# Recurrent branch of a hybrid block: products 512 and 256 wide, halves added on two engines

## The chip, the cores and the metric

The kernel runs on one core of a Trainium2 chip, for one layer at 256 tokens and width 2048, in float32. The metric is device time in microseconds. All weights come from HBM in each execution. Engines: TensorE (PE) multiplies, VectorE (DVE) and ScalarE (ACT) work elementwise, SyncE (SP) issues nearly all transfers.

## The reference, cut to what matters

```python
def rg_lru(x, w_a, b_a, w_i, b_i, lam):
    r = sigmoid(einsum('btnd,nde->btne', xb, w_a) + b_a)
    i = sigmoid(einsum('btnd,nde->btne', xb, w_i) + b_i)
    log_a = (8.0 * r) * log_sigmoid(lam)
    a = exp(log_a)
    b = sqrt(-expm1(2.0 * log_a)) * (i * x)
    return scan(h_t = a_t * h_{t-1} + b_t)

z = rmsnorm_mod(x) @ w_in         # q, kc, vc, ks, vs, kw, vw, gates, lx, ly, ga, gb
o_a = nsa_attention(...)
u = causal_dwconv(lx, conv_w, conv_b)            # 4 taps
o_b = gelu(ly) * rg_lru(u, w_a, b_a, w_i, b_i, lam)
merged = sigmoid(ga) * (o_a @ proj_a) + sigmoid(gb) * (o_b @ proj_b)
x = x + g1 * (merged @ w_out)
x = x + g2 * conv_glu_ffn(rmsnorm_mod(x))
```

The six vectors that scale, shift and gate come from `silu(c) @ ada_w`, 12288 columns wide.

## The kernel before, in words

Every float32 product is made of three products of rounded parts. A weight tile is split into `hi`, its rounded copy, written by ScalarE (L107), and `lo`, the rest, written by VectorE (L108); the activations lie in SBUF as 512 columns, 256 of rounded values and then 256 of the rest. The sum is hi with both halves and lo with the first. Weights come in tiles `raw` of 128 x 2048 (1 MB, four buffers, loaded through `stage`, L97, on SP's queue in program order). Each is split in two parts of 1024 columns; `hi` and `lo` have three buffers each. One such part is called a half below.

`dense_pair` (L114), used in the up projection, multiplies hi with all 512 columns at once and lo with 256, and a reduction adds the two halves of the accumulator. `dense_pair1` (L172), used for the recurrent branch, makes three products 256 wide (L185, L187, L188) into half a bank, so that one bank holds the two finished tiles of a call and no addition is needed. There are four banks `P` (tag "d").

The program order near the change is as follows. After the projections for attention, eight calls of `dense_pair1` compute `lx` (L721), each followed by an attention unit while any is left and by two pieces of the modulation (`filler(2)`, L726; a piece is one 1 MB load of `ada_w` and one 2048-wide VectorE operation, L234). ScalarE copies each accumulator into `lx` (L722), whose four buffers are the slots C4 to C7; C7 holds a tile of attention until its last unit.

Then come four blocks of the recurrence (L731), 512 channels each. A block makes the convolution `u` on VectorE (L746 the first tap, L749 the others), the gate products (L751, L753), sigmoids (L757, L758), a multiplication by -4 log_sigmoid(lam) on VectorE (L759), tanh (L761), exp (L762) and square root (L763) on ScalarE, three VectorE operations (L764 to L766), and the scan (L768). Two calls of `dense_pair1` per block then compute `ly`; ScalarE takes gelu from the accumulator into the slot of `u` (L773), VectorE multiplies with the scan's result (L774), and the product is split into `oB` (L777, L778).

The merge (L787) multiplies attention and recurrence by `proj_a` and `proj_b` in four groups of columns, with two fillers per product in the first group and four in the others (L803).

A scheduler orders each engine's instructions by a timeline of its own. `tc.high_priority` moves instructions forward, `tbl` keeps the order of ScalarE's functions that need tables, and the loads stay in program order. What an engine runs is the fixed order that results: an instruction that waits holds up those behind it.

## Time and profile before

| | us |
|---|---|
| median of three runs | 1794.22 (1793.13 to 1794.91) |
| the profiled execution | 1792.45 |
| its span, first to last instruction | 1790.7 |
| attention's last units and `lx`, about | 318 to 465 |
| recurrence and `ly`, about | 465 to 592 |
| merge, from | 592 |

In the profile, "PE P L188 <- DVE lo L108: 0.8, 2, 0.7" reads: TensorE's instructions of line 188 waited for VectorE's line 108 for 0.8 us in all, twice, at most 0.7. In a list of groups the columns are line, engine, operation, tiles and shapes, count, then busy time in us and mean duration in ns, then the idle time of the engine before it. In a timeline they are start, duration, engine, line. In the rows of the instruction order there is no time.

### The profile page before, as it was taken

The numbers are of one execution on the slowest core, as the hardware profiler recorded it, in microseconds if no ns is written. First come the engines' busy times: TensorE is split into PE (matmuls) and PEld (weight loads), VectorE is DVE, ScalarE is ACT, GpSimd is POOL, SyncE is SP. The second block draws the span as 40 slices with busy tenths as digits, with TensorE's granted clock in tenths as the row PEclk, the third lists the DMA queues.
The fourth block names the chain that finished last, engine by engine and source line by source line (L and its number), as shares of the span: only waits on it lengthen the run. The fifth ranks groups of instructions, "written<-read, shape, count | busy, mean of one in ns | idle before, by whom it ended". The sixth has DMA issues, their size and how long they took to land.

```text
span 1790.7 us, 25736 instructions
## 1 busy us (share of the span) xinstructions
PE 1769.6 (99%) x10254; PEld 1544.8 (86%) x10254; DVE 1350.7 (75%) x1978; ACT 883.1 (49%) x1204; POOL 0.2 (0%) x4
## 2 busy tenths in 40 slices
PE   8999999999999999999999999999999999999998
PEld 7899898888999888888888998888888888888886
DVE  7999897998698766767665997888555666777555
ACT  5644464655578444444445644444433444444443
POOL 0000000000000000000000000000000000000000
PEclk8999999999999999999999999999999999999999
DMA  9989864665555867777775566777655555555552
GB/s 348 379 330 364 289 248 157 236 212 208 215 177 223 305 236 291 284 292 282 293 265 198 186 233 237 282 282 282 236 193 200 193 188 190 188 188 188 189 193 112
DMA packets 64344, 429.50 MB, mean 240 GB/s; under 512 B 7104, under 2 KB 7392, under 8 KB 15840
## 3 DMA queue, kind: packets, MB, share of 16 engines
q1 hardware_dynamic: 63936, 427.08, 66.1%
q8 instruction: 80, 1.31, 0.3%
q10 hardware_dynamic: 288, 0.79, 0.1%
q14 instruction: 40, 0.33, 0.0%
HBM read 425.72 MB, written 2.11 MB: 239 GB/s over the span
## 4 chain that ended last, share of the span: by engine, by line
PE 93%; DVE 3%; DMA 1%; ACT 1%; issue 1%; SPq 0%; DVEq 0%; ACTq 0%
PE P L130 26%; PE P L204 12%; PE P L205 12%; PE P L203 12%; PE P L187 3%; PE P L188 3%; PE P L185 3%; PE P L470 2%; PE P L471 2%; PE P L472 2%; PE P L149 1%; PE P L464 1%; PE P L148 1%; PE P L465 1%; PE P L150 1%; PE P L463 1%
## 5 line engine op out<-in xcount | busy, mean ns | idle before, releaser
L107 ACT ACTIVATE hi<-raw 128x1024 fp32r<-128x1024 f32 x588 | 622.1, 1060 | 764.2 <-PE P L205 320.8
L108 DVE TENSOR_TENSOR lo<-raw,hi 128x1024 fp32r<-128x1024 f32 x588 | 717.0, 1222 | 370.6 <-ACT hi L107 369.7
L130 PE MATMUL P<-h,hi 128*128 128x512 f32 x1344 | 463.9, 394 | 0.0
L130 PE MATMUL P<-h,lo 128*128 128x256 f32 x1344 | 366.4, 278 | 0.0
L130 PEld LDWEIGHTS P<-h,hi 128*128 128x128 f32 x1344 | 249.1, 188 | 54.9
L130 PEld LDWEIGHTS P<-h,lo 128*128 128x128 f32 x1344 | 252.4, 188 | 4.2
L234 DVE SCALAR_TENSOR_TENSOR raw<-raw,crow 128x2048 f32<-128x2048 f32 x64 | 146.2, 2284 | 3.3 <-DMA raw<-ada_w 3.1
L188 PE MATMUL P<-h,lo 128*128 128x256 f32 x512 | 147.6, 289 | 0.8 <-DVE lo L108 0.8
L187 PE MATMUL P<-h,hi 128*128 128x256 f32 x512 | 146.8, 287 | 0.0
L185 PE MATMUL P<-h,hi 128*128 128x256 f32 x512 | 146.8, 287 | 0.0
L470 PE MATMUL P<-h,hi 128*128 128x256 f32 x384 | 108.0, 285 | 0.0
L471 PE MATMUL P<-h,hi 128*128 128x256 f32 x384 | 107.9, 285 | 0.0
L472 PE MATMUL P<-h,lo 128*128 128x256 f32 x384 | 102.2, 283 | 0.0
L188 PEld LDWEIGHTS P<-h,lo 128*128 128x128 f32 x512 | 97.8, 191 | 1.8 <-DVE lo L108 1.4
L187 PEld LDWEIGHTS P<-h,hi 128*128 128x128 f32 x512 | 97.9, 191 | 1.4 <-issue 1.2
L185 PEld LDWEIGHTS P<-h,hi 128*128 128x128 f32 x512 | 97.9, 191 | 1.0 <-issue 0.7
L204 PE MATMUL P<-lo,ua 128*128 128x512 f32 x240 | 93.4, 389 | 0.0
L205 PE MATMUL P<-hi,ua 128*128 128x512 f32 x240 | 93.4, 389 | 0.0
L203 PE MATMUL P<-hi,ua 128*128 128x512 f32 x240 | 83.6, 389 | 0.0
L204 PE MATMUL P<-lo,h 128*128 128x512 f32 x192 | 75.4, 393 | 0.2 <-DVE lo L108 0.2
L205 PE MATMUL P<-hi,h 128*128 128x512 f32 x192 | 74.9, 390 | 0.0
L470 PEld LDWEIGHTS P<-h,hi 128*128 128x128 f32 x384 | 74.2, 193 | 0.5 <-issue 0.4
(285 smaller groups left out, 3131.0 us busy)
## 6 DMA issues: line engine op xcount, KB each, us to landing
raw<-w_up SPq DMA_DIRECT2D x96, 1024.0 KB, 4.8
raw<-ada_w SPq DMA_DIRECT2D x94, 1024.0 KB, 4.9
raw<-w_down SPq DMA_DIRECT2D x48, 1024.0 KB, 4.8
raw<-w_lru SPq DMA_DIRECT2D x32, 1024.0 KB, 4.9
raw<-w_proj SPq DMA_DIRECT2D x32, 1024.0 KB, 5.1
raw<-w_gates SPq DMA_DIRECT2D x24, 1024.0 KB, 6.4
raw<-w_out SPq DMA_DIRECT2D x16, 1024.0 KB, 4.9
raw<-w_kv SPq DMA_DIRECT2D x24, 512.0 KB, 7.2
```

Of the source, the lines that this page charges most:

```text
L107: A.activation(hi[:, :n], raw[:, lo_col:lo_col + n], AF.Copy)
L108: V.tensor_tensor(lo[:, :n], raw[:, lo_col:lo_col + n], hi[:, :n].bitcast(F32), op=ALU.subtract)
L130: PE.matmul(ps[f][:, 0:256] if w else ps[f], hl[w][:, k * 256 + f * 128:k * 256 + f * 128 + 128], r[:, 0:256] if w else r, start=(kt == 0 ...
L185: PE.matmul(o, hi[:, sl], r[:, 0:256], start=(kt == 0 and f == 0), stop=False, skip_group_check=True)
L187: PE.matmul(o, hi[:, sl], r[:, 256:512], start=False, stop=False, skip_group_check=True)
L188: PE.matmul(o, lo[:, sl], r[:, 0:256], start=False, stop=(kt == n - 1), skip_group_check=True)
L203: PE.matmul(ps[j], xh, hi[:, w], start=(kt == 0), stop=False, skip_group_check=True)
L204: PE.matmul(ps[j], xh, lo[:, w], start=False, stop=False, skip_group_check=True)
L205: PE.matmul(ps[j], xl, hi[:, w], start=False, stop=(kt == n - 1), skip_group_check=True)
L234: V.scalar_tensor_tensor(raw, raw, 1.0, row, op0=ALU.mult, op1=ALU.mult, accum_out=modc[:, c:c + 1])
L470: PE.matmul(o, hi[:, sl], h1[:, kt, 0:256], start=first and f % 2 == 0, stop=False, skip_group_check=True)
L471: PE.matmul(o, hi[:, sl], h1[:, kt, 256:512], start=False, stop=False, skip_group_check=True)
```

## The change

Line numbers in the text on the changed kernel are its own; behind the change of `dense_pair1` they lie one to seven above those of before.

- `dense_pair1` makes one product 512 wide (L184) and one 256 wide (L185) per tile into a bank of its own, two banks per call.
- `add_halves`, new, copies the second half of each bank on ScalarE (L192) and adds the first on VectorE (L193), at high priority.
- `lx` lies in C4, C5, C6 and D0; the gelu of `ly` has a slot of its own (C0 to C7, later that of `oB`) and not that of `u`; the temporaries of the recurrence move to other slots.
- The convolution's first tap moves to ScalarE (L753).
- The multiplication by -4 log_sigmoid(lam) goes into the scale of tanh (L766), and exp becomes four instructions with a scale of 8 log_sigmoid(lam) (L768); `lsp8` (L606) is that vector.
- The gelu works in SBUF, and the product with the scan's result is written over the latter.
- After each `lx` call one or two fillers run, 12 in all and not 16; in the merge's first group four per product and not two.

```diff
         def dense_pair1(pieces, rhs):
-            p = bank()
+            ps = [bank(), bank()]
...
-                        o = p[:, f * 256:f * 256 + 256]
...
-                            PE.matmul(o, hi[:, sl], r[:, 0:256], start=(kt == 0 and f == 0), stop=False,
+                            PE.matmul(ps[f], hi[:, sl], r, start=(kt == 0), stop=False, skip_group_check=True)
+                            PE.matmul(ps[f][:, 0:256], lo[:, sl], r[:, 0:256], start=False, stop=(kt == n - 1),
                                       skip_group_check=True)
-                            PE.matmul(o, hi[:, sl], r[:, 256:512], start=False, stop=False, skip_group_check=True)
-                            PE.matmul(o, lo[:, sl], r[:, 0:256], start=False, stop=(kt == n - 1),
-                                      skip_group_check=True)
-            return p
+            return ps
+
+        def add_halves(dst, ps):
+            with tc.high_priority(200):
+                for f in range(2):
+                    A.activation(dst[:, f], ps[f][:, 256:512], AF.Copy)
+                    V.tensor_tensor(dst[:, f], ps[f][:, 0:256], dst[:, f], op=ALU.add)
...
+            lsp8 = lz
+            V.tensor_scalar(lsp8, ls, 8.0, None, op0=ALU.mult)
...
-        lx = [big.tile([128, 4, T], F32, tag="C%d" % (4 + n), name="lx") for n in range(4)]
+        lx = [big.tile([128, 4, T], F32, tag=t_, name="lx") for t_ in ("C4", "C5", "C6", "D0")]
...
-            A.activation(lx[pr // 2][:, 2 * (pr % 2):2 * (pr % 2) + 2],
-                         pl.rearrange("p (f t) -> p f t", f=2), AF.Copy)
+            add_halves(lx[pr // 2][:, 2 * (pr % 2):2 * (pr % 2) + 2], pl)
             if units:
                 attention(*units.pop(0))
-            filler(2)
+            filler(1 + pr % 2)
...
-                    V.tensor_scalar(uf, x, col("lcw", 48 + b), col("lcb", b), op0=ALU.mult, op1=ALU.add)
+                    A.activation(uf, x, AF.Identity, bias=col("lcb", b), scale=col("lcw", 48 + b))
...
-                V.tensor_scalar(r[:, n], r[:, n], lsm4[:, b:b + 1], None, op0=ALU.mult)
-                if n % 2:
-                    tbl(A.activation(tt[:, n - 1:n + 1], r[:, n - 1:n + 1], AF.Tanh))
-            tbl(A.activation(r, r, AF.Exp, scale=-2.0))
+                tbl(A.activation(tt[:, n], r[:, n], AF.Tanh, scale=lsm4[:, b:b + 1]))
+            for n in range(4):
+                tbl(A.activation(r[:, n], r[:, n], AF.Exp, scale=lsp8[:, bt * 4 + n:bt * 4 + n + 1]))
             tbl(A.activation(tt, tt, AF.Sqrt))
...
-                gl = u[:, 2 * h:2 * h + 2]
-                tbl(A.activation(gl, pl.rearrange("p (f t) -> p f t", f=2), AF.Gelu_apprx_tanh))
-                V.tensor_tensor(gl, gl, iu[:, 2 * h:2 * h + 2], op=ALU.mult)
+                gl, hs_ = big.tile([128, 2, T], F32, tag="C%d" % pr, name="gl"), iu[:, 2 * h:2 * h + 2]
+                add_halves(gl, pl)
+                tbl(A.activation(gl, gl, AF.Gelu_apprx_tanh))
+                V.tensor_tensor(hs_, gl, hs_, op=ALU.mult)
...
-                filler(2 if n == 0 else 4)
+                filler(4)
```

Two places of the order on the engines that the prediction speaks of: on ScalarE, in a block of the recurrence, where the splits of weights (`hi<-raw`) stand between its functions (`lt`; L761 tanh, L762 exp, L763 root, L773 gelu), before, in the third block:

```order
L107 ACTIVATE hi<-raw 128x1024 x2
L761 ACTIVATE lt<-lt 128x512
L762 ACT_TABLE_LOAD
L762 ACTIVATE lt<-lt 128x1024
L763 ACT_TABLE_LOAD
L763 ACTIVATE lt<-lt 128x1024
L107 ACTIVATE hi<-raw 128x1024
L773 ACT_TABLE_LOAD
L773 ACTIVATE lt<-P 128x512
```

and in the first block of the changed kernel (L768 exp, L753 first taps of a later block, L769 root, L780 gelu, L764 and L765 sigmoids):

```order
L768 ACT_TABLE_LOAD
L768 ACTIVATE lt<-lt,lz 128x256 x3
L753 ACTIVATE lt<-lx,cols 128x256 x4
L768 ACTIVATE lt<-lt,lz 128x256
L769 ACT_TABLE_LOAD
L769 ACTIVATE lt<-lt 128x1024
L780 ACT_TABLE_LOAD
L780 ACTIVATE gl<-gl 128x512 x2
L764 ACT_TABLE_LOAD
L764 ACTIVATE lt<-lru_r,cols 128x256
L765 ACTIVATE lt<-lru_i,cols 128x256
L107 ACTIVATE hi<-raw 128x1024
```

The gelus (L780) and the next block's first sigmoids (L764, L765), each with a table load, and four first taps moved ahead of the split. On SP's queue (loads by tile and source) the pieces of `ada_w` in the merge's first group become four per product; before:

```order
L53 DMA raw<-w_proj 128x2048 x4
L53 DMA raw<-ada_w 128x2048 x2
L53 DMA raw<-w_proj 128x2048 x4
L53 DMA raw<-ada_w 128x2048 x2
L53 DMA raw<-w_gates 128x2048 x4
```

and after:

```order
L53 DMA raw<-w_proj 128x2048 x4
L53 DMA raw<-ada_w 128x2048 x4
L53 DMA raw<-w_proj 128x2048 x4
L53 DMA raw<-ada_w 128x2048 x4
L53 DMA raw<-w_gates 128x2048 x4
```

The four pieces that left the `lx` loop stand behind the two products of this group.

## The prediction

> **What bounds the kernel now.** I read the page first, then busy time by stage, then the waits of TensorE, and last the timelines of TensorE and ScalarE where the change acts.

> ```profile
> span 1790.7 us, 25736 instructions
> PE 1769.6 (99%) x10254; PEld 1544.8 (86%) x10254; DVE 1350.7 (75%) x1978; ACT 883.1 (49%) x1204; POOL 0.2 (0%) x4
> PE 93%; DVE 3%; DMA 1%; ACT 1%; issue 1%; SPq 0%; DVEq 0%; ACTq 0%
> ```

> TensorE is the bound nearly everywhere. Busy time on that engine is modelled, so what matters is the pitch from one product's start to the next. The stages, with columns us, PE, PEld, DVE, ACT, POOL, clock, DMA share and GB/s, are the recurrence's inputs beside attention (318 to 465), the recurrence proper (465 to 592), and the first part of the merge:

> ```profile
> 318.00:465.00 147.00, 146.51 (x1023) 124.24 (x1022) 131.14 (x356) 87.81 (x217) 0.00 (x0) 1.00 0.60 211
> 465.00:592.00 127.00, 126.18 (x948) 120.71 (x947) 104.05 (x142) 93.56 (x123) 0.00 (x0) 1.00 0.59 213
> 592.00:650.00 58.00, 58.00 (x261) 48.02 (x261) 38.91 (x45) 24.36 (x26) 0.00 (x0) 1.00 0.72 267
> ```

> VectorE is 89% busy in the first of them, ScalarE 74% in the second. TensorE waits there, in all, for this:

> ```profile
> PE tp L695 <- ACT pcT L667: 0.5, 1, 0.5
> PE P L188 <- DVE lo L108: 0.8, 2, 0.7
> ```

> These are 1.3 us, so removing waits can bring little. ScalarE, on the other side, still has slack in the recurrence: it mostly waits for TensorE to free one of the three `hi` buffers.

> ```profile
> ACT hi L107 <- PE P L187: 17.3, 13, 3.3
> ```

> **The products.** One pair of tiles now takes three 256-wide products, and afterwards one of 512 and one of 256, the form that the up projection (L130) has today. Columns are start, duration, line and operation:

> ```profile
> 524.48 0.28 PE L185 MATMUL P<-h,hi 128*128 128x256 f32 x1
> ...
> 525.92 0.28 PE L185 MATMUL P<-h,hi 128*128 128x256 f32 x1
> 1400.13 0.39 PE L130 MATMUL P<-h,hi 128*128 128x512 f32 x1
> ...
> 1403.94 0.40 PE L130 MATMUL P<-h,hi 128*128 128x512 f32 x1
> ```

> From 524.48 to 525.92 are four rounds of three: 1.44/4 = 0.360 us. From 1400.13 to 1403.94 are eleven rounds of two: 3.81/11 = 0.3464 us. The columns streamed are the same; what goes is one instruction, 13.6 ns. There are 512 rounds (16 calls, 16 row tiles, 2 halves), so the products save 512 x 0.0136 = 7.0 us, all on the path. [...]

> The two accumulators per call take two of the four banks, so a call's first product waits for the sums of the call before last. A call lasts 32 x 0.3464 = 11.1 us and each sum is put ahead in both queues: I cost that at nothing, and at 1 us a call if the cover goes.

> **VectorE.** The rows for what goes and comes (busy, then mean ns):

> ```profile
> L234 DVE SCALAR_TENSOR_TENSOR raw<-raw,crow 128x2048 f32<-128x2048 f32 x64 | 146.2, 2284 | 3.3 <-DMA raw<-ada_w 3.1
> L746 DVE TENSOR_SCALAR lt<-lx,cols 128x256 f32<-128x256 f32 x16 | 5.8, 407 | 0.3 <-PE s L673 0.3
> L759 DVE TENSOR_SCALAR lt<-lt,lsm 128x256 f32<-128x256 f32 x16 | 5.3, 347 | 2.1 <-ACT lt L757 1.9
> L161 DVE TENSOR_TENSOR gp<-P,rB 128x256 f32<-128x256 f32 x6 | 2.4, 416 | 0.0
> ```

> Gone are 5.8 and 5.3 us, added are 32 sums at 0.416 = 13.3 us, and four modulation pieces (9.1 us) leave the attention stage for the merge. In the attention stage VectorE is relieved by some 5 us (16 sums against four pieces and a few taps). That is worth the 0.5 us wait there, no more.

> **ScalarE is where I see the price.** It gets 32 copies, 16 first taps and 16 separate exponentials. How they are ordered matters more than their sum. In the two pieces of its queue shown with the change, a split of weights (`hi`, L107) came right behind the root; after, the closing split stands behind the root, two gelus and the next block's first sigmoids, and four taps stand among the exponentials. Two more such runs follow, in blocks 1 and 2. The rows that price them:

> ```profile
> 543.37 0.61 ACT L761 ACTIVATE lt<-lt 128x512 f32<-128x512 f32 x1
> 544.00 1.28 ACT L762 ACT_TABLE_LOAD   x1
> 545.29 1.06 ACT L762 ACTIVATE lt<-lt 128x1024 f32<-128x1024 f32 x1
> 546.36 1.28 ACT L763 ACT_TABLE_LOAD   x1
> 547.65 1.06 ACT L763 ACTIVATE lt<-lt 128x1024 f32<-128x1024 f32 x1
> 548.62 1.04 ACT L107 ACTIVATE hi<-raw 128x1024 fp32r<-128x1024 f32 x1
> 549.68 1.28 ACT L773 ACT_TABLE_LOAD   x1
> L349 ACT ACTIVATE nt<-xbuf,modc 128x256 f32<-128x256 f32 x14 | 8.2, 588 | 0.0
> L298 ACT ACTIVATE h<-nt,modc 128x256 fp32r<-128x256 f32 x18 | 8.7, 500 | 5.5 <-DVE nt L304 5.1 <-DVE nt L876 0.3
> L906 ACT ACTIVATE ua<-fv 128x256 fp32r<-128x256 f32 x32 | 12.1, 418 | 1.5
> L757 ACT ACTIVATE lt<-lru_r,cols 128x256 f32<-128x256 f32 x16 | 7.7, 479 | 0.9 <-PE lru_r L751 0.9
> L814 ACT ACTIVATE mg<-turn 128x256 fp32r<-128x256 f32 x16 | 5.2, 377 | 2.8 <-PE turn L812 2.8
> ```

> A table load stands 1.29 us before its successor (544.00 to 545.29), a 1024-wide operation 0.97 (547.65 to 548.62), so a queued activation about 0.1 us less than its duration. Taking 0.1 off the others: a tap, which has a bias and a scale per partition as L349 has, 0.49; a tanh or exp with a scale per partition 0.40 as L298 (bounds 0.32 by L906, which has none, and 0.49 by L349); a sigmoid 0.37; a copy of a half sum 0.28 by L814. The rows shown of after, the closing split included, so take 12.5 us, against 6.3 for those of before (543.37 to 549.68). [...]

> TensorE's cover is three split halves: 16 products, 8 x 0.3464 = 2.77 us each. The last of the three is handed over 1 us after the buffer came free. The plain sum over the stretch from the last attention product to the end of the third run, ten splits by the order of after:

> - ScalarE: 10 splits at 0.97, 10 table loads at 1.29, 23 sigmoids at 0.37, 24 tanh and exp at 0.40, 12 taps at 0.49, 3 roots at 0.97, 6 of 512 at 0.53, 7 copies at 0.28, one output copy 0.5: 9.7 + 12.9 + 8.5 + 9.6 + 5.9 + 2.9 + 3.2 + 2.0 + 0.5 = 55.2 us.
> - TensorE meanwhile: 12 halves, 33.3 us; 20 gate products and 4 of attention's:

> ```profile
> 521.77 0.60 PE L751 MATMUL lru_r<-lt,raw 128*128 128x256 f32 x2
> 522.21 0.59 PE L753 MATMUL lru_i<-lt,raw 128*128 128x256 f32 x2
> 470.56 3.44 PE oT L703 x8
> ```

> A gate product is two records, 0.44 us (521.77 to 522.21); attention's four are the 3.44. Together 33.3 + 8.8 + 3.4 = 45.5, less the 1 us of the first hand-over, 44.5.

> The difference, 10.7 us, is time in which TensorE has no split weights. With the bounds of the new activations (24 at 0.32 or 0.49, taps at 0.40) it is 7.7 to 12.9; sums that wait in VectorE's queue behind a late `lo` may add up to 4. The same reckoning for before gives some 28 us of ScalarE work in ten splits, far below TensorE's; only the 6.3 us run comes near three halves, and the larger of the two waits, 0.7 us, is what it costs. In the last block the runs are 4.6, 2.6, 2.8 and 6.7 us against halves of 2.77: 16.7 against 11.1 and the cover of some 4: I put 2 us (0 to 3.5).

> **The moved pieces.** As SP's queue shows, four loads of 1 MB join the merge's first group, ahead of loads of weights. In the 58 us from 592 VectorE is busy 38.91, 67%, and with 9.1 us more 83%; transfers go from 267 GB/s to about 267 + 4.2 MB/58 us = 340. Both leave room, less in the group itself, which is shorter. I take 0.5 us (0 to 2.3).

> **Sum.** Against the profiled execution, 1792.45 us with a span of 1790.7: -7.0 (products) -1.3 (waits that go) +10.7 +2 +0.5 = +4.9, so 1797.4. The median of the three runs, 1794.22, lies 1.8 above that execution: **1799.2 us**.

> **The rivals.**

> - *Faster: the runs on ScalarE are covered.* It holds if the three halves and the gate products hide each run, so that the second stage waits no more than now. For it: the 17.3 us that ScalarE itself waits for TensorE today. Against it: that slack lies between runs, and 55.2 against 44.5 leaves none. It decides where all new waits together stay below 4.7 us (8.3 less 3.6). With none, 1794.2 - 8.3 = 1786. Chance 0.15.
> - *No change: the shortfall is half of my sum.* New activations at their cheap bound, the last block covered: -8.3 + 7.7 = -0.6, so 1793 to 1795. Chance 0.22.
> - *Slower still: VectorE's order adds to it.* Half sums, taps of the next block and a modulation piece stand ahead of a `lo` whose products are already late, and the merge starts with VectorE behind: -8.3 + 12.9 + 4 + 2.3 = +11, so 1805. Chance 0.13.

> **How the numbers follow.** The forecast has 0.50, at 1799.2. About 0.2% (3.6 us) is what a measurement of this kernel can tell from no change: 1790.6 to 1797.8. Faster is the first rival, 0.15; same the second and nothing else, 0.22; slower the rest, 0.63. The range leaves out half of the first rival and the top of the last: 1788 to 1806.

> **What would show it.** Pitch of L184 to L184 at 0.346 us. Waits of TensorE for `hi` L107 or `lo` L108 in the second stage near 10 us in three or four places, each behind a run of table loads on ScalarE, where before there were 0.8. No wait for the sums at L193. The attention stage shorter by 4 us. If those waits stay below 3 us in all, the forecast is wrong and the first rival right.

## The result, and the profile after

The changed kernel takes **1814.71 us** (median of four runs, 1811.90 to 1817.39), the kernel before, run beside it, 1794.05 (1793.13 to 1794.91): ratio 1.0119, 95% interval 1.0107 to 1.0132, 20.7 us slower. The direction was forecast, at 1799.2 us with a range from 1788 to 1806; the size was not.

The profiled execution of the change is its slowest run, 1817.39 us. The head and the chain of waits on its page, which answer to the three lines of the prediction:

```profile
span 1815.6 us, 24767 instructions
PE 1776.4 (98%) x9742; PEld 1523.1 (84%) x9742; DVE 1352.6 (74%) x1979; ACT 899.5 (50%) x1264; POOL 0.2 (0%) x4
PE 84%; DVE 6%; ACT 4%; DMA 4%; issue 2%; SPq 0%; DVEq 0%; ACTq 0%
```

TensorE's share of the chain fell from 93% to 84%; VectorE, ScalarE and the transfers took its place. The same three stages (us, PE, PEld, DVE, ACT, POOL, clock, DMA share, GB/s):

```profile
318.00:465.00 147.00, 147.00 (x803) 115.07 (x802) 122.12 (x325) 86.07 (x210) 0.00 (x0) 1.00 0.57 205
465.00:592.00 127.00, 119.04 (x620) 98.91 (x619) 94.92 (x153) 102.06 (x178) 0.00 (x0) 0.96 0.50 177
592.00:650.00 58.00, 50.68 (x219) 40.86 (x218) 50.35 (x60) 26.71 (x30) 0.00 (x0) 0.97 0.76 288
```

TensorE now stands for 8.0 and 7.3 us in the second and third, and the clock, 1.00 before, is 0.96 and 0.97. Where the time went can be read from the first and the last start of the recurrent products, of before and then of after (instruction, count, duration in ns as least, median and most, then first and last start):

```profile
L185 PE MATMUL P<-h,hi x512: 277/283/681, 321.9 to 584.0; 128*128 128x256 f32 x171
```

```profile
L184 PE MATMUL P<-h,hi x512: 387/396/796, 326.1 to 602.4; 128*128 128x512 f32 x171
```

The stretch of these products, from the first start to the last, grew from 262.1 to 276.3 us, **+14.2**. From its end to the first up product (983.4 and 1008.3) it is 399.4 and 405.9, **+6.5**; what follows takes 807.3 in both. Together that is 20.7 us, as much as the medians differ. The two profiled executions are 24.9 us apart; the other 4.2 us are a later start of the stretch. TensorE's instructions ahead of it are the same in both kernels, and the start came between 321.8 and 326.1 in the executions below (at 324.4 and 325.4 in two kernels that differ from before only further on), so it is no part of the loss.

What TensorE waits for from 465 to 650 us (in all, times, longest):

```profile
PE P L184 <- ACT hi L107: 7.9, 4, 3.2
PE P L206 <- ACT hi L107: 4.2, 2, 2.2
PE P L185 <- DVE lo L108: 2.5, 2, 2.0
PE P L207 <- DVE lo L108: 0.7, 1, 0.7
```

One of the two at L206 (2.2 us, at 598) and all at L184 and L185 belong to the recurrence: **12.6 us**, 10.1 of it for `hi` and 2.5 for `lo`. The longest stands behind this run on ScalarE (start, duration):

```profile
515.76 1.07 ACT L107 ACTIVATE hi<-raw 128x1024 fp32r<-128x1024 f32 x1
...
517.52 1.28 ACT L768 ACT_TABLE_LOAD   x1
518.81 1.31 ACT L768 ACTIVATE lt<-lt,lz 128x256 f32<-128x256 f32 x3
520.02 2.06 ACT L753 ACTIVATE lt<-lx,cols 128x256 f32<-128x256 f32 x4
...
524.87 1.28 ACT L780 ACT_TABLE_LOAD   x1
526.16 1.15 ACT L780 ACTIVATE gl<-gl 128x512 f32<-128x512 f32 x2
527.33 1.28 ACT L764 ACT_TABLE_LOAD   x1
...
529.35 1.05 ACT L107 ACTIVATE hi<-raw 128x1024 fp32r<-128x1024 f32 x1
```

```profile
527.01 0.28 PE L185 MATMUL P<-h,lo 128*128 128x256 f32 x1
530.46 1.22 PE L184 MATMUL P<-h,hi 128*128 128x512 f32 x2 [3.17 <-ACT hi L107]
```

From the start of one split to the start of the next are 13.6 us. TensorE used up its three split halves and stood 3.2 us. This is the run in the prediction, with the tap, the gelus and the next sigmoids in it. What the prediction does not have is in the windows of 3.41 us around such waits:

```profile
526.64:530.05 3.41, 0.66 (x4) 0.31 (x2) 1.79 (x3) 3.38 (x6) 0.00 (x0) 1.00 0.00 0
530.05:533.46 3.41, 3.00 (x7) 2.38 (x8) 3.02 (x5) 3.41 (x8) 0.00 (x0) 0.50 0.20 38
550.53:553.94 3.41, 1.42 (x7) 0.89 (x6) 3.41 (x5) 3.40 (x6) 0.00 (x0) 1.00 0.34 135
553.94:557.35 3.41, 3.41 (x12) 2.93 (x11) 3.41 (x7) 3.39 (x10) 0.00 (x0) 0.50 0.82 291
```

TensorE is busy 0.66 and 1.42 us in the first of each pair, and its granted clock is 0.50 in the whole of the next. There are five such windows at half clock, four in the recurrence and one in the merge, and none in the kernel before between its start and its end (1.00 from 26.1 to 1787.4 us). A round of L184 and L185 takes 0.64 us in them (548.42 to 549.06) and 0.353 at full clock (509.53 to 511.65, six rounds). By that, as an estimate, a window costs up to 1.5 us (3.41 x (1 - 0.353/0.64)); in the four of the recurrence TensorE is busy for 13.2 us, so they cost 5.9.

Why the functions stand in such runs was not isolated. What the profile shows is that the products run ahead of attention: the last copy of attention's result (`oA`) starts at 474.0 before and 508.2 after:

```profile
L707 ACT ACTIVATE oA<-oT x8: 578/597/604, 327.3 to 474.0; 128x512 fp32r<-128x512 f32 x8
```

```profile
L712 ACT ACTIVATE oA<-oT x8: 578/597/598, 331.4 to 508.2; 128x512 fp32r<-128x512 f32 x8
```

Before, the accumulator of a `ly` call was held until its gelu, which stands behind the block's other functions on ScalarE; in the change the sums free it. In the second stage ScalarE is busy for 102.06 us and not 93.56. Neither is the loss by itself: in a kernel below with the change's products and no block functions (`e12_after_bare`) that copy starts just as late, and no product of the stretch waits,

```profile
L712 ACT ACTIVATE oA<-oT x8: 578/597/598, 328.7 to 505.6; 128x512 fp32r<-128x512 f32 x8
```

and in `e5_mended`, with all functions, it starts at 508.1, ScalarE is busy for 100.26 us of that stage, and the stretch is shorter than before.

### The profile page after: what moved, and what is told of

It is laid out like the page before. It is cut to its first block, busy times and chain, and to the rows that moved or that the text cites. A ratio compares the mean times of both kernels' runs of the same rounds, so it can differ in the third digit from the quotient of the medians.

```text
span 1815.6 us, 24767 instructions
## 1 busy us (share of the span) xinstructions
PE 1776.4 (98%) x9742; PEld 1523.1 (84%) x9742; DVE 1352.6 (74%) x1979; ACT 899.5 (50%) x1264; POOL 0.2 (0%) x4
## 4 chain that ended last, share of the span: by engine, by line
PE 84%; DVE 6%; ACT 4%; DMA 4%; issue 2%; SPq 0%; DVEq 0%; ACTq 0%
PE P L130 26%; PE P L207 11%; PE P L208 11%; PE P L206 11%; PE P L184 5%; PE P L185 2%; DVE lo L108 2%; PE P L473 2%; PE P L475 2%; DMA raw<-ada_w 2%; PE P L474 2%; PE P L149 1%; PE P L148 1%; PE P L150 1%; PE s L678 1%
## 5 line engine op out<-in xcount | busy, mean ns | idle before, releaser
L107 ACT ACTIVATE hi<-raw 128x1024 fp32r<-128x1024 f32 x588 | 621.4, 1060 | 766.7 <-PE P L208 305.0
L108 DVE TENSOR_TENSOR lo<-raw,hi 128x1024 fp32r<-128x1024 f32 x588 | 717.4, 1223 | 369.3 <-ACT hi L107 368.4
L130 PE MATMUL P<-h,hi 128*128 128x512 f32 x1344 | 463.9, 394 | 0.0
L130 PE MATMUL P<-h,lo 128*128 128x256 f32 x1344 | 367.1, 278 | 0.0
L130 PEld LDWEIGHTS P<-h,hi 128*128 128x128 f32 x1344 | 249.6, 188 | 54.6
L130 PEld LDWEIGHTS P<-h,lo 128*128 128x128 f32 x1344 | 252.6, 188 | 4.2
L184 PE MATMUL P<-h,hi 128*128 128x512 f32 x512 | 188.0, 409 | 7.9 <-ACT hi L107 7.9
L237 DVE SCALAR_TENSOR_TENSOR raw<-raw,crow 128x2048 f32<-128x2048 f32 x64 | 146.3, 2287 | 18.4 <-DMA raw<-ada_w 18.3
L185 PE MATMUL P<-h,lo 128*128 128x256 f32 x512 | 145.4, 291 | 2.5 <-DVE lo L108 2.5
L184 PEld LDWEIGHTS P<-h,hi 128*128 128x128 f32 x512 | 97.4, 193 | 28.6 <-ACT hi L107 9.2
L473 PE MATMUL P<-h,hi 128*128 128x256 f32 x384 | 108.2, 286 | 1.5 <-ACT hi L107 1.5
L474 PE MATMUL P<-h,hi 128*128 128x256 f32 x384 | 107.8, 285 | 0.0
L185 PEld LDWEIGHTS P<-h,lo 128*128 128x128 f32 x512 | 99.2, 194 | 6.2 <-DVE lo L108 3.4
L206 PE MATMUL P<-hi,ua 128*128 128x512 f32 x240 | 83.7, 390 | 0.0
L473 PEld LDWEIGHTS P<-h,hi 128*128 128x128 f32 x384 | 74.1, 193 | 2.4 <-ACT hi L107 1.9
L474 PEld LDWEIGHTS P<-h,hi 128*128 128x128 f32 x384 | 74.1, 193 | 0.0
L332 DVE SCALAR_TENSOR_TENSOR raw<-raw,crow 128x2048 f32<-128x2048 f32 x30 | 68.4, 2286 | 4.1 <-DMA raw<-ada_w 4.0
```

Of the source, the lines that this page charges most:

```text
L107: A.activation(hi[:, :n], raw[:, lo_col:lo_col + n], AF.Copy)
L108: V.tensor_tensor(lo[:, :n], raw[:, lo_col:lo_col + n], hi[:, :n].bitcast(F32), op=ALU.subtract)
L130: PE.matmul(ps[f][:, 0:256] if w else ps[f], hl[w][:, k * 256 + f * 128:k * 256 + f * 128 + 128], r[:, 0:256] if w else r, start=(kt == 0 ...
L184: PE.matmul(ps[f], hi[:, sl], r, start=(kt == 0), stop=False, skip_group_check=True)
L185: PE.matmul(ps[f][:, 0:256], lo[:, sl], r[:, 0:256], start=False, stop=(kt == n - 1), skip_group_check=True)
L206: PE.matmul(ps[j], xh, hi[:, w], start=(kt == 0), stop=False, skip_group_check=True)
```

## The experiments

Times are medians beside the kernel before on the same chip, with the ratio's interval. The last two columns, in us, are of one profiled execution each.

| kernel | us | ratio to before | products' stretch | to the first up product |
|---|---|---|---|---|
| e1_products_alone | 1806.02 | 1.0054 to 1.0084 | 274.2 | 398.8 |
| e2_tap_on_vector | 1808.29 | 1.0072 to 1.0102 | 267 | 409 |
| e3_exp_joined | 1813.23 | 1.0094 to 1.0128 | 277 | 405 |
| e4_fillers_back | 1808.96 | 1.0073 to 1.0103 | 276.8 | 398.4 |
| e5_mended | 1797.70 | 1.0013 to 1.0032 | 257.4 | 406 |
| e6_order_alone | 1807.99 | 1.0062 to 1.0096 | 261.5 | 414.4 |
| e7_tap_and_pieces | 1802.69 | 1.0033 to 1.0067 | 267 | 403 |
| e9_mended_vector | 1796.09 | 1.0009 to 1.0029 | 257.5 | 406 |
| e10_tap_on_gpsimd | 1793.87 | 0.9993 to 1.0011 | 257.2 | 404.7 |
| e13_spread_gpsimd | 1794.38 | 0.9993 to 1.0012 | 257.2 | 406 |
| e14_spread_vector | 1794.91 | 0.9998 to 1.0015 | 256.2 | 405 |
| e16_pieces_earlier | 1793.38 | 0.9990 to 1.0008 | 257.1 | 404.0 |

**One part alone, one part undone.** First the products' form put into the kernel before, with sums into the old places:

```diff
 (before, with dense_pair1 and add_halves of after)
-            A.activation(lx[...], pl.rearrange("p (f t) -> p f t", f=2), AF.Copy)
+            add_halves(lx[pr // 2][:, 2 * (pr % 2):2 * (pr % 2) + 2], pl)
-                tbl(A.activation(gl, pl.rearrange(...), AF.Gelu_apprx_tanh))
+                add_halves(gl, pl)
+                tbl(A.activation(gl, gl, AF.Gelu_apprx_tanh))
```

> Theory A (ScalarE's long runs of other work between two splits starve TensorE, and the clock falls after each such wait): only the products and their sums are changed here; by the order the longest run is one of 9.6 us, the others at most 6.6 as before. Products save 7 us, the one run costs 2 to 3: 1789 to 1792 us, waits of TensorE for hi or lo in the recurrence below 4 us, no clock drop in it. Theory B (the products' own form costs: two banks per call, sums on two engines): above 1800 us, with waits for the sums or at L184.

1806.02: theory A's number failed and B's came true, but the waits that B names, for a sum or at L184, are 1.3 us in all. The longest waits of TensorE, and the clock, say more:

```profile
PE P L206 <- ACT hi L107: 2.2, 1, 2.2
PE P L185 <- DVE lo L108: 2.1, 3, 1.3
PE lru_r L753 <- ACT p L688: 1.7, 1, 1.7
```

```profile
473.06:483.30 10.24, 8.52 (x24) 6.51 (x25) 6.71 (x24) 3.40 (x12) 0.00 (x0) 0.50 0.28 102
```

With the sums still in `u` and in attention's slots TensorE is held up at attention's end, and the clock stays at half for three windows there and one each at 524 and 593. So the form alone is not good either, and both theories were too simple. The freed slots are not needed for a loss: without them the stretch is nearly as long, with its waits in other places.

Then three parts of the change undone singly: the tap on VectorE again, the tanh and exponentials as before, the modulation pieces as before.

```diff
-                    A.activation(uf, x, AF.Identity, bias=col("lcb", b), scale=col("lcw", 48 + b))
+                    V.tensor_scalar(uf, x, col("lcw", 48 + b), col("lcb", b), op0=ALU.mult, op1=ALU.add)
```

> The changed kernel with the first tap back on VectorE. Theory A: the three long runs become 10.6, 8.6 and 7.9 us (from 13.1, 10.3 and 10.5), so the waits in the recurrence fall from 13.7 to about 5 us, with one or two clock drops: 1800 to 1805 us. Theory C (the modulation pieces moved into the merge are what costs): 1811 to 1815 us as in the changed kernel.

```diff
-                tbl(A.activation(tt[:, n], r[:, n], AF.Tanh, scale=lsm4[:, b:b + 1]))
-            for n in range(4):
-                tbl(A.activation(r[:, n], r[:, n], AF.Exp, scale=lsp8[:, bt * 4 + n:bt * 4 + n + 1]))
+                V.tensor_scalar(r[:, n], r[:, n], lsm4[:, b:b + 1], None, op0=ALU.mult)
+                if n % 2:
+                    tbl(A.activation(tt[:, n - 1:n + 1], r[:, n - 1:n + 1], AF.Tanh))
+            tbl(A.activation(r, r, AF.Exp, scale=-2.0))
```

> The changed kernel with the multiplication by -4 log_sigmoid back on VectorE, tanh 512 wide and exp 1024 wide. Theory A: runs of 13.3, 10.1 and 7.8 us, waits of 8 to 9 us and two or three clock drops: 1804 to 1810 us. Theory C: 1811 to 1815 us.

```diff
-            filler(1 + pr % 2)
+            filler(2)
-                filler(4)
+                filler(2 if n == 0 else 4)
```

> The changed kernel with 16 modulation pieces beside lx and two per product in the merge's first group, as before. ScalarE's runs between splits stand as in the changed kernel (13.1, 10.3, 10.5). Theory A: the recurrence keeps its waits of some 13 us; 1812 to 1815 us. Theory C: the merge's waits and clock drops go, 4 to 7 us: 1808 to 1811 us.

Undone, the tap gives 6.4 us back (in the profiled executions 9.4 in the stretch, with 3.3 lost in the merge), the exponentials 1.5 (within the scatter of the runs), the pieces 5.8. The first lies between the two theories, the other two are C's numbers, though with the pieces back the stretch stays as long as in the change, as A says: no single part cures the runs on ScalarE, and the pieces, put at 0.5 us, cost ten times that. Their price is seen in the change's merge, on ScalarE and VectorE:

```profile
637.93 1.06 ACT L107 ACTIVATE hi<-raw 128x1024 fp32r<-128x1024 f32 x1 [1.66 <-PE P L208]
646.96 2.01 ACT L107 ACTIVATE hi<-raw 128x1024 fp32r<-128x1024 f32 x2 [7.96 <-DMA raw<-w_gates]
```

```profile
640.50 1.22 DVE L108 TENSOR_TENSOR lo<-raw,hi 128x1024 fp32r<-128x1024 f32 x1
641.64 2.28 DVE L237 SCALAR_TENSOR_TENSOR raw<-raw,crow 128x2048 f32<-128x2048 f32 x1
...
644.46 2.29 DVE L237 SCALAR_TENSOR_TENSOR raw<-raw,crow 128x2048 f32<-128x2048 f32 x1 [0.46 <-DMA raw<-ada_w]
...
648.61 1.22 DVE L108 TENSOR_TENSOR lo<-raw,hi 128x1024 fp32r<-128x1024 f32 x1
```

The split waits 8 us for weights that stand in the queue behind the pieces' 1 MB loads (SP issues the four pieces from 625.9 on and these weights from 640.6), and four pieces in a row hold the `raw` buffers until VectorE has worked them off. TensorE waits 2.0 and 0.7 us there, and a window at half clock follows.

**Both together.** `e7_tap_and_pieces` has the edits of e2 and e4.

> The change with the first tap back on VectorE and the modulation pieces back where they were, ScalarE's order left to the scheduler (longest runs 10.3, 8.6 and 8.3 us). If the gains of the two single reversals add up (each took about 6 us off the change's 1814): 1801 to 1804. Theory A by the run lengths: three waits of 1 to 2.5 us, one or two drops of the clock: 1797 to 1804 us.

1802.69, as the two singly add up. The stretch is 267 us: in three places 8.7 to 10.7 us still pass from the start of one split to that of the next.

**The order alone.** Here nothing of the change is undone. A dependency without a semaphore makes certain block functions follow certain weight splits, which cuts the runs:

```diff
+        for which, nth, what, half in [(0, 0, 'exp', 47), (0, 0, 'sqrt', 48), (0, 0, 'gelu', 49), (1, 0, 'sig', 51), ...]:
+            fn = [f_ for b_, w_, f_ in fns if b_ == which and w_ == what][nth]
+            tc.add_manual_dep(fn.ins, splits[first_split + half].ins.name, NOSYNC, reason="split first")
```

> The change with nothing but ScalarE's order mended in the recurrence (groups of block functions made to follow certain splits; longest run 8.4 us instead of 13.1); tap on ScalarE, separate exps and moved modulation pieces stay. Theory A: the waits of 13.7 us fall to 2 to 5 and the four drops of the clock in the recurrence to none or one, the merge's wait of 3 us with its drop stays: 1796 to 1803 us. Theory B: no change from 1814 beyond 3 us. Theory C (the moved pieces carry most of the loss): 1808 to 1813.

```profile
L187 PE MATMUL P<-h,hi x512: 387/395/586, 324.3 to 585.8; 128*128 128x512 f32 x171
```

The stretch falls by 14.8 us to 261.5 and has no window at half clock, though 5 us of shorter waits are left in it. But the merge takes 8.5 us more: seven waits for `lo` (4.3 us), two for `hi` (3.3), two windows at half clock. The time, 1807.99, is above theory A's 1803 and at the edge of C's. Order is the cause in the recurrence, for nothing else was changed there; but the work that is put off then meets the merge, and ScalarE and VectorE need a place for it.

**Mended.** `e5_mended` joins the order, the edits of e2 and e4, and a free slot for the last block's tanh:

```diff
-                tt = big.tile([128, 4, T], F32, tag="C7", name="lt")
+                tt = big.tile([128, 4, T], F32, tag="C7", name="lt") if bt == 1 else l4[:, 0]
```

> The change with its first tap on VectorE, its modulation pieces where they were before, the last block's tanh slot moved from C7 to the half of D4 that blocks 0 and 2 use (so that the last sum does not wait for the last block), and ScalarE's order mended: each group of the block functions (sigmoids, exps, sqrt, gelus) is made to follow a certain weight split, so that no run of other ScalarE work between two splits is longer than 6.1 us (13.1 in the change). Theory A (TensorE starves behind long ScalarE runs, and the clock falls after the waits; the products themselves gain what their pitch says): no wait over 1 us in the recurrence, the clock at 1.00, recurrent products' stretch 255 to 259 us (before 262.2), 1784 to 1790 us. Theory B (the form of the products costs, whatever the order): above 1797. If ScalarE is short of time over the whole stretch whatever the order: waits of 0.5 to 1 us at many halves, 1790 to 1797.

The stretch is 257.4, as theory A expected, with no wait over 0.7 us. The time, 1797.70, is not A's but in B's range; B's reason, the form of the products, does not fit the shorter stretch. The merge has the loss: three waits for VectorE, 4.1 us in all, and one window at half clock behind the longest:

```profile
588.15 2.29 DVE L240 SCALAR_TENSOR_TENSOR raw<-raw,crow 128x2048 f32<-128x2048 f32 x1
...
590.36 1.23 DVE L111 TENSOR_TENSOR lo<-raw,hi 128x1024 fp32r<-128x1024 f32 x1
```

```profile
591.64 0.74 PE L210 MATMUL P<-lo,oA 128*128 128x512 f32 x1 [2.27 <-DVE lo L111]
```

So VectorE's order was mended too (pieces earlier in the recurrence, later in the merge), then the tap went to GpSimd:

```diff
-                filler(2 if pr % 4 == 0 else 0)
+                with tc.high_priority(300):
+                    filler(2 if pr < 2 else 0)
-                filler(4)
+                filler(4 if n or s else 0)
```

> The mended kernel (tap on VectorE, ScalarE's groups behind certain splits, last tanh off C7) with VectorE's order mended too: the four modulation pieces of the second part of the recurrence follow the first two of its products, and the two that ran at the head of the merge come a product later. In the mended kernel TensorE waited 2.4 and 1.6 us at the head of the merge for splits on VectorE that stood behind such pieces of 2.29 us, and the clock fell for one window. Theory A (waits for late splits, on whichever engine, and the clock's fall after them): those waits and the fall go, 1790 to 1793 us. Theory B (the mended kernel's remaining loss is the sums' own work, VectorE being full): 1796 to 1799.

1796.09, the low end of theory B; a wait of 2.3 us with a window at half clock behind it is still there, from 599, now for a split on ScalarE.

```diff
-                    V.tensor_scalar(uf, x, col("lcw", 48 + b), col("lcb", b), op0=ALU.mult, op1=ALU.add)
+                    nc.gpsimd.tensor_scalar(uf, x, col("lcw", 48 + b), col("lcb", b), op0=ALU.mult, op1=ALU.add)
```

> The kernel with VectorE's order mended, and the first tap (16 operations) on GpSimd, which does nothing else. If VectorE's time is what is short in the second part: another 1 to 3 us less than with the tap on VectorE, 1787 to 1791. If a slower tap on GpSimd holds the block functions back, or GpSimd slows VectorE: the same or up to 4 us more.

1793.87: 2.2 us less than with the tap on VectorE, as the first case says, but not its 1787 to 1791; no window at half clock, level with before. Two more spread the last block's functions over more splits and give attention priority (`tc.high_priority(1000)` around it); in the second, nine groups also follow one split later than in the first:

> The kernel with the first tap on GpSimd and both orders mended, but the last block's groups on ScalarE spread over three more splits (into the merge's first product), and attention's instructions given priority, so that the block functions start a split earlier; the longest run between two splits is 5.4 us, and no ten in a row are over TensorE's time for them. The kernel with the tap on GpSimd still waited 4 us at the head of the merge, behind splits 62 to 69 of ScalarE with 3.3 to 6.0 us each. Theory A (what is left is ScalarE's pace against TensorE's, which an order can meet): those waits go, the merge's stretch falls from 404.5 to 400, the time to 1787 to 1790 us, 0.2% to 0.3% faster than before. Theory B (the sums' own work on ScalarE and VectorE is the rest, whatever the order): 1792 to 1796.

> The same with the first tap on VectorE, nothing on GpSimd. Theory A: two waits of about 1 us more than with the tap on GpSimd: 1788 to 1793 us. Theory B: 1795 to 1798.

1794.38 and 1794.91: theory B's numbers, or just below. The last moves two pieces from the merge into the recurrence:

> The kernel with the tap on GpSimd and the spread orders, with two of the four modulation pieces behind the merge's first pair of products moved back into the recurrence (behind its products 3 and 4, counted from 0). In it TensorE waited 4.1 us in seven places between 598 and 630 us for the second halves of splits on VectorE, next to these pieces of 2.29 us. Theory A (late splits alone): those waits go to under 1 us, the merge's stretch from 405.9 to 401 or 402, 1789 to 1791 us (0.1% to 0.2% under before). Theory B (the sums' added work is the rest): the waits come back elsewhere, 1793 to 1796.

1793.38, 0.9990 to 1.0008. The products' stretch is 5.0 us shorter than before, and the merge gives 4.6 of it back, 2.4 of that in waits for VectorE:

```profile
L187 PE MATMUL P<-h,hi x512: 387/395/796, 326.0 to 583.1; 128*128 128x512 f32 x171
```

```profile
PE P L210 <- DVE lo L111: 2.4, 5, 1.1
```

The time is theory B's, and waits are left in another place. That the sums' added work is the reason, as B has it, no run isolates. No kernel tried here beats the one before by more than its interval.

**The products without the block functions.** These two leave out the sigmoids, tanh, exponentials, roots, scans and gelus, so that nothing starves TensorE; a copy of the taps' result stands in for them:

```diff
-            for n in range(4):
-                b, (gr_, gi_), sl = ...
-                ... (all up to the scans)
+            V.tensor_copy(iu, u)
```

> The kernel before without its block functions: sigmoids, tanh, exp, square root, scan and gelu are left out (one copy of the taps' result and plain copies stand in their place), so that ScalarE and VectorE have time to spare; what is computed is not the reference. Only to be compared with the next one. Theory A: TensorE sets the pace, the recurrent products' stretch is 255 to 260 us, 1785 to 1791 us.

> The change without its block functions, in the same way. Theory A (the products gain what their pitch says, 512 rounds x 0.0136 us, once nothing starves them): 6 to 9 us less than the kernel before without them, in the recurrent products' stretch; no wait over 1 us and no fall of the clock there; the merge's moved pieces may still cost 2 to 6 us. Theory B (the form of the products or the added halves cost): no gain in that stretch, or a loss.

```profile
L185 PE MATMUL P<-h,hi x512: 277/283/681, 325.4 to 585.9; 128*128 128x256 f32 x171
```

```profile
L184 PE MATMUL P<-h,hi x512: 387/395/586, 323.4 to 578.5; 128*128 128x512 f32 x171
```

260.5 against 255.1 us: the form gains 5.4 us, a little less than the 6 to 9 expected, and theory B of its price is out. There is no wait over 0.5 us and no fall of the clock in either stretch; the merge of the second, with its moved pieces, still waits 2.1 us and has one window at half clock. The times, of one run each, are 1794.47 (1785 to 1791 was expected) and 1791.43 us. Against its bare form the kernel before itself loses only 1.6 us.

**The price of a run by itself.** In the kernel before, in the down projection, where ScalarE does nothing but split, extra activations in a row were put between two splits:

```diff
+                    if extra and ip == 3 and half == 0:
+                        for _ in range(extra):
+                            more = A.activation(junk[0], junk[0], AF.Copy)
+                            tc.add_manual_dep(more.ins, last.ins.name, NOSYNC, reason="in a row")
+                            last = more
```

> The kernel before with 8, 9, 10 and 11 extra 1024-wide ScalarE activations in a row between two splits at four places of the first down projection, and 12, 14 and 16 at three of the second; nothing else runs on ScalarE there. Each takes about 0.97 us. Theory A: TensorE lives on three split halves (3 x 2.8 us = 8.4 us), so that the wait behind a run is its length with the split, less about 8.3: 0.4, 1.4, 2.4, 3.3, 4.3, 6.2 and 8.2 us; and the granted clock falls to half for one window of 3.4 us after each wait of 1.4 us or more and not after the 0.4 (if the fall goes with the length of the wait, for two windows or more after the longest). If the clock's fall in the change has another cause: no fall behind any of these. Time: 1793 + 26 of waits + 1.7 for each window at half clock, about 1829.

> The kernel before with extra ScalarE activations in a row between two splits of the down projections again: 7, 8, 8, 8 in the first, 8, 8 and 9 in the second. With 8 of them TensorE had waited 2.7 and 0.7 us with no fall of the clock, with 9 it had waited 3.8 us and the clock fell for two windows of 3.41 us. If what decides is the wait's length: none of the five runs of 8 makes the clock fall. If the windows stand on a fixed raster and the clock falls after one in which TensorE stood for 2.0 us or more (as the waits of all traces so far read): some of the five runs of 8 make it fall and some don't, as the 3.4 us of each are divided between two windows, the 7 (2.3 us) only where nearly all of it lies in one, the 9 nearly always.

Behind 8 and 9 of them in the first kernel TensorE stood:

```profile
1270.00 0.39 PE L209 MATMUL P<-hi,ua 128*128 128x512 f32 x1
1272.91 0.73 PE L207 MATMUL P<-hi,ua 128*128 128x512 f32 x2 [2.52 <-ACT hi L109]
...
1306.27 0.39 PE L209 MATMUL P<-hi,ua 128*128 128x512 f32 x1
1310.27 1.22 PE L207 MATMUL P<-hi,ua 128*128 128x512 f32 x2 [3.61 <-ACT hi L109]
```

Each further activation adds 1.09 us, its own length, so past some 6 us of run (8 x 1.09 = 8.7, less the wait of 2.5) each of the seven waits, 43.8 us in all, is the run's excess, one for one. The waits are 2.1 to 3.0 us longer than I expected, since the cover is those 6 us with the split on top and not 8.3, and an activation in this row took 1.09 and not 0.97 (each works on the result of the one before; whether that is why was not tested). With that, and with two to four windows at half clock behind each of the six longer waits (the mean granted clock of the execution is 0.983), the time is 1857.77 us and not 1829. The second kernel took 1830.34 (one run each). The windows around the first two waits, and then, of the second kernel, around its 7 and its first two 8:

```profile
1268.89:1272.30 3.41, 1.50 (x7) 0.92 (x5) 0.00 (x0) 3.35 (x4) 0.00 (x0) 1.00 1.01 423
1272.30:1275.72 3.42, 2.28 (x9) 1.58 (x10) 2.83 (x3) 2.46 (x3) 0.00 (x0) 1.00 0.23 96
1306.44:1309.85 3.41, 0.22 (x1) 0.00 (x0) 0.00 (x0) 3.35 (x4) 0.00 (x0) 1.00 0.00 0
1309.85:1313.26 3.41, 2.96 (x6) 1.95 (x7) 3.02 (x3) 2.26 (x3) 0.00 (x0) 0.50 0.00 0
1313.26:1316.68 3.42, 3.42 (x9) 2.65 (x9) 0.48 (x1) 0.48 (x1) 0.00 (x0) 0.50 0.87 302
```

```profile
1272.03:1275.44 3.41, 1.97 (x9) 1.18 (x7) 0.52 (x1) 3.38 (x4) 0.00 (x0) 1.00 1.00 423
1309.58:1312.99 3.41, 1.24 (x4) 0.76 (x5) 1.79 (x2) 3.41 (x4) 0.00 (x0) 1.00 0.00 0
1312.99:1316.40 3.41, 3.41 (x9) 2.64 (x9) 1.71 (x2) 0.08 (x1) 0.00 (x0) 0.50 0.49 144
1347.13:1350.54 3.41, 0.90 (x3) 0.46 (x4) 1.45 (x2) 3.41 (x4) 0.00 (x0) 1.00 0.00 0
1350.54:1353.95 3.41, 3.41 (x9) 2.65 (x10) 2.05 (x2) 0.42 (x1) 0.00 (x0) 0.50 0.42 118
```

In the first kernel the 8 fell across two windows (busy 1.50 and 2.28) and the clock stayed; in the second the same 8, five times, lay mostly in one (busy 1.24 and 0.90 in the two shown), and each time the next window ran at half clock. That some of the five would be spared did not come true; the one that was spared is that of the first kernel. Behind the 7 (busy 1.97) the clock stayed. In these two kernels it was not the wait's length alone, 2.52 us behind the 8 that was spared and 2.53 behind the first of the others, but how much of it lay in one window. Behind 9 (the two windows shown) and more the clock fell for two windows or more.

## Why the prediction was right in its direction and wrong in its size

| step, as the prediction put it | forecast | measured |
|---|---|---|
| products, 512 rounds | -7.0 | -5.4 (bare pair) |
| waits that go | -1.3 | -1.6 (before against its bare form) |
| ScalarE's shortfall, and the last block | +10.7 +2 | +8.0 +4.6 (waits in the recurrence) |
| the clock after the waits | not in the sum | +5.9 (four windows, by the rounds' pace in them) |
| the moved pieces | +0.5 | +6.5 (the merge) |
| sum | +4.9 | +18.0 of 20.7 |

The step on **ScalarE** held in kind: runs between two splits that three split halves can't cover, in the places forecast, each behind table loads. It was tested in both directions: e6, with nothing but the order changed, took 14.8 us out of the stretch, and added runs in another stage made TensorE wait by their length. That 12.6 us were measured for 12.7 is partly luck. Up to the third run the waits are 8.0 us for 10.7, inside the bounds of 7.7 to 12.9; in the last block they are 4.6 for 2, above the 3.5 that it was given.

The step on **the products** was right in kind and too large. The round is not 0.346 us as in the up projection:

```profile
509.53 0.40 PE L184 MATMUL P<-h,hi 128*128 128x512 f32 x1
...
511.65 0.40 PE L184 MATMUL P<-h,hi 128*128 128x512 f32 x1
```

Six rounds in 2.12 us are 0.353 here; over all 512 rounds the 5.4 us of the bare pair are 10.5 ns a round and not 13.6.

**What failed** is, first, a term that is not in the sum: "10.7 us is time in which TensorE has no split weights" was taken as the whole price of such time. TensorE works on at half clock afterwards: four windows, 5.9 us by the pace in them. No whole idle window is needed: here one with TensorE busy for 1.42 us was enough, and one with 1.66, so waits of 2.0 us must be priced as well.

Second, the step "**the moved pieces** ... I take 0.5 us (0 to 2.3)". It reckoned VectorE's and the transfers' mean load over 58 us. What counted was the group itself: four loads in a row ahead of weights in one queue, a split 8 us late, then the clock. Putting the pieces back took 5.8 us off the time.

Third, "no wait for the sums at L193" came true, but "the attention stage shorter by 4 us" did not: attention's last copy starts 34 us later. That the products would run ahead of attention was not seen; whether this is what put the functions into runs stays open. Some 2.7 us of the 20.7 are not accounted for. An estimate for about half of it: a wait is counted from the modelled end of the product before, 0.28 us behind the start of a 256-wide one, whose successor starts 0.12 us behind it when nothing waits (three in a round of 0.360), so that each of the nine waits in the two stages is some 0.16 us longer than its row says.

Of the rivals, the slower one named VectorE's order; the waits for its `lo` are 2.5 us in the recurrence, and once ScalarE's order is mended most of TensorE's waits in the merge are behind VectorE (in all the mended kernels but e9). There the mended kernels end: the form's 5 us are lost again in the merge, about half of them as such waits (2.4 of 4.6 us in e16). Whether another placing of VectorE's work could keep them was not settled.

## What to carry to other kernels

Before taking a wait away, ask what it kept in step: here the products ran ahead of attention without it, and the order of ScalarE's work that came with the change held up the weight splits on which TensorE lives (that the one brought the other was not shown). Count the work between two splits in the order of the queue, not the engine's mean load, and compare it with what the buffers cover. Where TensorE would stand for some 2 us or more within 3.41 us, as in the windows ahead of the five at half clock here (1.75 to 2.75 us), add some 1.5 us for the clock; and let bulk loads and long VectorE operations not stand in a row ahead of weights.
